# Loads behind the last value stores, one group's first turns ahead of its last scores, and eight row norms beside other units: one edit of a two-layer decoder step

## The chip, the cores and the metric

The kernel runs on one core of one Trainium2 chip. The core has a matrix engine (PE, with its weight loads listed apart as PEld), a vector engine (DVE), a scalar engine (ACT), a general engine (POOL) and a sync engine (SP) that here only issues DMAs. The metric is the time of one execution in device microseconds. The kernel before took 2337.07 us, the median of three runs (2333.03 to 2337.43).

## The reference

One inference step of a two-layer decoder runs over a prompt of 2048 rows and over 8 sequences of 4 new rows with 2048 cached rows each. Model width is 1024. Cut to what the change touches:

```python
# layer 0: HGRN2 heads (a) beside forgetting attention (b), one input and one output projection
proj = rmsnorm(x, norm_even) @ w_in
qa, fa, ia, ga, qb, kb, vb, gb, fb = split(proj)
c = cumsum(log_sigmoid(fb + b_fox))
logits = q @ k.T * scale + c[t] - c[s]          # 4 heads, 128 wide, causal over 2048 rows
o_b = softmax(logits) @ v * silu(gb)            # the new rows attend to paged k, v in the same way
x = x + concat([o_a, o_b]) @ w_out

# layer 1: gated linear attention, 4 heads
h = rmsnorm(x, norm_odd)
q, k, v, g, r = split(h @ w_in_odd)             # here r gives the decay: log_sigmoid(r @ w_gate + b) / 16
o = head_norm(chunked_linear_attention(q, k, v, decay)) * silu(g)
y = rmsnorm(x + o @ w_out_odd, final_norm)
```

The step also returns the keys and values of the prompt and of the new rows, and the final states.

## The kernel before

Products of full precision are made of three half-precision ones: each operand is split in a high and a low half, and `mm3` (lines 603 to 607) issues high by high, high by low and low by high. So a line of PE work shows three lines L605, L606 and L607. Splitting an operand takes one ACT instruction for the high half and one DVE instruction for the low half. The prompt is worked through in two halves of 1024 rows.

The program is written as Python generators. `mux(a, ta, b, tb)` draws from two of them in turn, so that each has used the same part of its planned time `ta` or `tb`; `drain` runs one to its end. A scheduler then sets the order of the instructions on each engine from a simulated timeline. `tc.issue_after(i)` gives it a bound: what is issued inside stands behind instruction `i`. On the chip each engine works its own list in that order, SP too: a DMA issue that waits holds up all later ones.

Three places are touched.

*End of layer 0's input projections.* The last unit computes the values of heads 2 and 3 for the second half. For each pair of row tiles (named by half, head pair and tile: 112 is the pair of tiles 2 and 3) `ev` in `mk_bkv` writes a float tile `Bv`, split halves `Bvs` (ACT line 1048, DVE line 1049), stores `Bvs` to `vd` from SP (line 1063) and `Bv` to the output from POOL (line 1066). Both tiles come from a pool of four buffers, so that the last pair, 116, takes the buffers of 112 and can be written when the stores of 112 have landed.

*Prompt attention, `fox_prompt` (lines 1341 to 1473).* Its 16 groups are 4 heads by 4 stretches of 512 query rows. `loads(h, G)` brings q, k (a transposing DMA), a bias strip, v and a gate strip (names such as `q2_02`: head 0, stretch 2). `scores` makes, for each of four blocks `b` of 128 rows, the products `s` (PE), adds the bias and takes the maximum `mx` (DVE line 1391), the exponentials (ACT line 1399) and the scaling (POOL line 1407). `values` transposes the scores in turns (PE line 1427), splits each turn into `th` (ACT line 1434) and `tl` (DVE line 1435) and multiplies by v into `fo`; it keeps two turns ahead. While group j is scored, the values of group j-1 are drawn, a quarter of them behind each block. The loads of group j+1 are asked for behind block 0 of group j. The last group has no group behind it: its values come by themselves, in two column halves. The decode attention, which reads pages of the cache (`pgcache_fox_k`, transposed by PE line 1546), runs beside the prompt's.

*Layer 1, `phase_odd`.* Units 0 to 7 are layer 0's output projection, and units 8, 9 and 10 are Cv0, Cqk0 and Cg0: head 0's projections for v (with the 16 columns of r), q and k, and gate, over the first half. `three(0, 11)` then runs the recurrences of heads 0 to 2, each beside three later units. Layer 1's rows must be normed before they are projected. `prep(hf)` does this for the 8 row tiles of a half by `norm_store` (lines 521 to 563): load `x1r` from `x1d` (SP line 540), squares `nsq` (ACT line 546), a reciprocal root `rsr` (DVE and POOL), the gain (POOL line 548), the high half (ACT line 553), the low half (DVE line 554), and a store to `xs` (SP line 555). For the second half the `x1r` tiles have two buffers (`yr`), and the loads are bound to stand behind `last_turn`, the last of the transposing DMAs by which `norm_fetch` brings the first half's normed rows from `xs` to `act` (SP line 574). The projection Cv0 writes one row tile at a time to three PSUM buffers; each is free when ACT (line 1884, `vC`) and DVE (`rh`, `rt`) have read it. The end of this part reads:

```python
            self.norm_fetch(act, 0, dense(7, 8))
            fetched(11)
            drain(dense(8, 11))
            drain(mux(prep(1), 10000.0, three(0, 11), 240000.0))
```

Of the kernel before, what the change touches and what calls it, by code (L numbers as in the profile page):

```python
# [111 lines left out]
def drain(g):  # L112
    for _ in g:
        pass
# [11 lines left out]
class Kern:  # L126
# [788 lines left out]
    def even_half(self, hf, act, wpool, wp, pps, npool, S):  # L915
# [104 lines left out]
        def mk_bkv(hp, which):  # L1020
            wide = which == "v" and hp == 0
            width = 260 if wide else 256

            def run(W):
                cs = slice(hp * 256, hp * 256 + 256)
                held = []
                if hf == 0:
                    self.fox_scale(which, hp)

                def ev(ps, g, cnt, m):  # L1030
                    c = sc(f"B{which}{hp}")[:m, 2:3]
                    if wide:
                        tt = hf * 8 + g if m == P else NPG
                        nc.vector.scalar_tensor_tensor(self.lf[:m, tt], ps[:, 0, 256:260], c, self.bfox[:m], ALU.mult,
                                                       ALU.add)
                    if g % 2 == 0:
                        held[:] = [wp.tile([P, 2, 256], F32, tag="c2", name=f"B{which}{hf}{hp}{g}")]
                        if m == P:
                            held.append(wp.tile([P, 512], F32, tag="c2", name=f"B{which}s{hf}{hp}{g}").bitcast(
                                F16).rearrange("p (g h x d) -> p g h x d", g=2, h=2, x=2))  # L1040
                    t = held[0]
                    nc.vector.tensor_scalar(t[:m, g % 2 : g % 2 + cnt], ps[:, :, :256], c, None, ALU.mult)
                    if m == P:
                        u = held[1]
                        for j in range(cnt):
                            src = ps[:, j, :256].rearrange("p (h d) -> p h d", h=2)
                            hi, lo = (u[:, g % 2 + j, :, x] for x in range(2))
                            nc.scalar.activation(hi, src, AF.Copy, scale=self.cu[which, hp])
                            nc.vector.scalar_tensor_tensor(lo, src, self.cu[which, hp], hi, ALU.mult, ALU.subtract)  # L1049
                    if m < P:  # L1050
                        dst = o[f"fox_{which}_s"][0].rearrange("b t h d -> (b t) (h d)")[:, cs]
                        nc.sync.dma_start(dst, t[:m, 0])
                        if which == "v":
                            nc.sync.dma_start(self.vs[:, cs], t[:m, 0])
                    elif (g + cnt) % 2 == 0:
                        if which == "v":
                            x = (hf * 4 + g // 2) * 2 + hp
                            nc.vector.tensor_reduce(self.vmax[:, x : x + 1], t, mybir.AxisListType.XY, ALU.max,
                                                    apply_absolute_value=True)
                        g0 = g // 2 * 2  # L1060
                        pg = hf * 8 + g0
                        dst = {"k": self.kd, "v": self.vd}[which][hf][g0 * P : (g0 + 2) * P, 2 * hp : 2 * hp + 2]
                        nc.sync.dma_start(dst.rearrange("(g s) h x d -> s g (h x d)", s=P),
                                          u.rearrange("p g h x d -> p g (h x d)"))
                        dst = o[f"fox_{which}_p"][0, 0, pg : pg + 2].rearrange("g s h d -> s g (h d)")[:, :, cs]
                        (nc.gpsimd if (hf, hp, which) == (1, 1, "v") else nc.sync).dma_start(dst, t)
                    if which == "k" and m < P:
                        pk = pps.tile([P, 2, 256], F32, tag="gr", name=f"BkT{hf}{hp}{g}")
                        for j in range(2):
                            nc.tensor.transpose(pk[:, j, :m], t[:m, 0, j * P : (j + 1) * P], self.ident[:m, :m])  # L1070
                        ks = wp.tile([P, 2, 256], F32, tag="c2", name=f"BkS{hf}{hp}{g}")
                        nc.scalar.activation(ks[:, :, :m], pk[:, :, :m], AF.Copy, scale=self.fsc["k", hp][0])
                        nc.sync.dma_start(self.ks[2 * hp : 2 * hp + 2].rearrange("h p t -> p h t"), ks[:, :, :m])

                yield from self.proj_tm(pps, act, W, hf, ev, f"B{which}{hf}{hp}", width)

            cols = [({"k": 2560, "v": 3072}[which] + hp * 256, 256)] + ([(4096, 4)] if wide else [])
            U[f"B{which}{hp}"] = unit(cols, f"B{which}{hp}", run)
# [262 lines left out]
    def fox_prompt(self, fx, pps, caus):  # L1341
# [65 lines left out]
                nc.gpsimd.tensor_scalar(lt[:, :w], lt[:, :w], nm[:, 1:2], 2.0**14, ALU.mult, ALU.mult)  # L1407
            return L

        def values(h, G, rows, po, b1, b2):  # L1410

            ns, per = 4 * G + b2, 4 // (b2 - b1)
            c1, c2 = b1 * P, b2 * P
            alone = self.sample_done

            def turn(j):


                tag = "kt" if alone and j % 2 else "t"
                pt = pps.tile([P, 512], F32, tag=tag, name=f"pt{h}{G}{b1}{j}")  # L1420
                w, parts = 0, []
                for s in range(j * per, min(j * per + per, ns)):
                    b0 = max(b1, s - 4 * G)
                    w = max(w, b0 * P if per == 1 else 0)
                    parts.append((s, w, b0 * P))
                    for b in range(b0, b2):
                        nc.tensor.transpose(pt[:, w : w + P], rows[b][s // 4][0][:, (s % 4) * P : (s % 4 + 1) * P],  # L1427
                                            self.ident)
                        w += P
                th = fx.tile([P, 512], F16, tag="th", name=f"th{h}{G}{b1}{j}")  # L1430
                tl = fx.tile([P, 512], F16, tag="tl", name=f"tl{h}{G}{b1}{j}")
                a = parts[0][1]
                self.turns.append((
                    nc.scalar.activation(th[:, a:w], pt[:, a:w], AF.Copy),  # L1434
                    nc.vector.tensor_tensor(tl[:, a:w], pt[:, a:w], th[:, a:w], ALU.subtract)))  # L1435
                return th, tl, parts

            nj = -(-ns // per)
            ahead = [turn(j) for j in range(min(2, nj))]
            for j in range(nj):  # L1440
                if j + len(ahead) < nj:
                    ahead.append(turn(j + len(ahead)))
                th, tl, parts = ahead.pop(0)
                for s, a, c0 in parts:
                    vv = [x[:, s % 4] for x in V[h, s // 4]]
                    self.last_pe = self.mm3(po[:, c0:c2], vv, [x[:, a : a + c2 - c0] for x in (th, tl)], s == 0,
                                            s == ns - 1)
                yield sum(c2 - c0 for _, _, c0 in parts) * 2.1
            y = fx.tile([P, 512], F32, tag="y", name=f"fy{h}{G}{b1}")
            nc.vector.scalar_tensor_tensor(y[:, c1:c2], po[:, c1:c2], self.v_undo[h // 2], SG[h, G][:, c1:c2], ALU.mult,  # L1450
                                           ALU.mult)
            nc.gpsimd.dma_start(self.yT[0][NH + h][:, G * 512 + c1 : G * 512 + c2], y[:, c1:c2])
# [4 lines left out]
        for j, (h, G) in enumerate(groups):  # L1457
            rows = []
            for b in range(4):
                rows.append((yield from scores(h, G, b)))  # L1460
                if j + 1 < len(groups) and b == 0:
                    loads(*groups[j + 1])
                for _ in range(ns // 4):
                    c = next(pv, None)
                    if c:
                        yield c
            yield from pv
            po = pps.tile([P, 512], F32, tag="o", name=f"fo{h}{G}")
            if j + 1 < len(groups):
                pv, ns = values(h, G, rows, po, 0, 4), 4 * (G + 1)  # L1470

        yield from values(h, G, rows, po, 0, 2)
        yield from values(h, G, rows, po, 2, 4)

    def strips(self, makers, sources):

# [497 lines left out]
    def phase_odd(self):  # L1974
# [4 lines left out]
        with pool("act2", side="right") as ap, pool("w2", side="right") as w0, pool("yr2", side="right") as y0, \  # L1979
# [34 lines left out]
            def dense(a, b):  # L2014
                return self.staged(units, a, b)
# [4 lines left out]
            def three(hf, a):  # L2020
                for h in range(3):
                    yield from recur(hf, h, a + 3 * h)
# [70 lines left out]
            drain(mux(prep(0), 11500.0, dense(4, 7), 63000.0))  # L2093
            self.norm_fetch(act, 0, dense(7, 8))
            fetched(11)
            drain(dense(8, 11))
            drain(mux(prep(1), 10000.0, three(0, 11), 240000.0))
            fetched(23)
            self.norm_fetch(act, 1)
            drain(recur(0, 3, 20))  # L2100
# [95 lines left out]
```

## Time and profile before

| what | value |
|---|---|
| median of three runs | 2337.07 us (2333.03 to 2337.43) |
| the profiled execution | 2338.06 us |
| its span | 2336.2 us (so 1.9 us lie around it) |
| granted PE clock, mean | 0.991 |
| PE busy | 2250.3 us, 96% |
| DVE busy | 1448.0 us, 62% |
| ACT busy | 1076.2 us, 46% |
| POOL busy | 768.7 us, 33% |

Times inside the execution are in microseconds from the start of its span. A row of the timeline gives the start, the duration, the engine, the line of the kernel, the operation, the tile written and the tiles read, and in brackets how long the engine had been idle and what ended that. SPq rows are the issues of DMAs; when a DMA lands is told apart. A row of waits gives the instruction that waited, what it waited for, the total, the number of times and the longest.

### The profile page before, as it was taken

To read this page: it belongs to the slowest core of one execution; us is meant where nothing else is said; L and a number is where in the kernel's file an instruction comes from. 1 tells how busy PE (TensorE), PEld (TensorE's weight loads), DVE (VectorE), ACT (ScalarE), POOL (GpSimd) and SP (SyncE) were. 2 spreads that over 40 slices of the span, in tenths; PEclk is the share of its full clock that TensorE was granted. 3 is DMA by queue.
4 is the path that set the end of the run, shared out by engine and by line. 5 is a ranking of instruction groups with operands and counts; after the bars stand their busy time and mean duration, and the time that the engine had idled before them with its cause. 6 is when DMAs were issued, how large, how long until landed. Compare 5 with 4: busy or idle time off the path is not lost.

```text
span 2336.2 us, 58122 instructions
## 1 busy us (share of the span) xinstructions
PE 2250.3 (96%) x23060; PEld 1604.1 (69%) x23060; DVE 1448.0 (62%) x3313; ACT 1076.2 (46%) x2360; POOL 768.7 (33%) x818
## 2 busy tenths in 40 slices
PE   7999999999999989999999999999899999999998
PEld 5667667864655876665545888777677666666887
DVE  7766577537655748667767445366675655557554
ACT  6434344333333326555656543546545545545343
POOL 2333324112212214223335445144552432322232
PEclk9999999999999999999999999999999999999999
DMA  7232334765441278877882968523233431115554
GB/s 201 66 93 67 94 106 152 182 170 138 147 136 43 89 178 268 247 234 221 271 249 73 341 198 261 141 84 119 75 113 86 126 104 58 46 58 163 167 188 150
DMA packets 375665, 344.87 MB, mean 148 GB/s; under 512 B 107633, under 2 KB 322994, under 8 KB 375394
## 3 DMA queue, kind: packets, MB, share of 16 engines
q1 hardware_dynamic: 373250, 334.54, 47.8%
q0 software_dynamic: 2144, 6.62, 0.8%
q8 instruction: 181, 2.97, 0.5%
q14 instruction: 90, 0.74, 0.1%
HBM read 244.54 MB, written 79.63 MB: 139 GB/s over the span
## 4 chain that ended last, share of the span: by engine, by line
PE 78%; DVE 8%; DMA 4%; ACT 3%; issue 2%; POOL 2%; SPq 2%; POOLq 0%; DVEq 0%; ACTq 0%
PE pt_o L605 4%; PE pt_o L607 4%; PE pt_o L606 4%; PE pkt L1546 2%; PE pt L1427 2%; PE pt_Cv L605 2%; PE pt_Cv L606 2%; PE pt_Cv L607 2%; PE sc L1605 1%; PE pv L1684 1%; PE pf_Ag L607 1%; PE pf_Ag L606 1%; PE pf_Ag L605 1%; PE pf_Bq L607 1%; PE pf_Bq L606 1%
## 5 line engine op out<-in xcount | busy, mean ns | idle before, releaser
L605 PE MATMUL pt_o<-w_o,act 128*128 128x256 f16 x1024 | 279.7, 273 | 2.3 <-ACT sg1C L662 2.3
L607 PE MATMUL pt_o<-w_o,act 128*128 128x256 f16 x1024 | 279.6, 273 | 0.9 <-POOL act L1785 0.9
L606 PE MATMUL pt_o<-w_o,act 128*128 128x256 f16 x1024 | 279.6, 273 | 0.0
L605 PEld LDWEIGHTS <-act 128*128 128x128 f16 x2304 | 226.7, 98 | 37.4 <-issue 4.1
L606 PEld LDWEIGHTS <-act 128*128 128x128 f16 x2304 | 226.8, 98 | 32.9 <-issue 3.6
L607 PEld LDWEIGHTS <-act 128*128 128x128 f16 x2304 | 226.8, 98 | 31.4 <-issue 1.9
L606 PE MATMUL pt_Cv<-w_Cv,act 128*128 128x256 f16 (+1 forms) x512 | 141.3, 276 | 0.0
L605 PE MATMUL pt_Cv<-w_Cv,act 128*128 128x256 f16 (+1 forms) x512 | 141.3, 276 | 0.0
L607 PE MATMUL pt_Cv<-w_Cv,act 128*128 128x256 f16 (+1 forms) x512 | 141.2, 276 | 0.0
L772 POOL TENSOR_TENSOR kA<-kA,fA 128x512 f32<-128x512 f32 (+1 forms) x56 | 77.9, 1392 | 186.2 <-PE gl_A L738 140.2
L772 POOL TENSOR_TENSOR kC<-kC,fC 128x512 f32<-128x512 f32 (+1 forms) x56 | 83.9, 1498 | 153.9 <-PE gl_C L738 107.8
L1407 POOL TENSOR_SCALAR L<-L,nm 128x512 f32<-128x512 f32 (+3 forms) x160 | 99.5, 638 | 104.6 <-DVE nm L1403 44.5
L1399 ACT ACTIVATE L<-L,nm,kc 128x512 f32<-128x512 f32 (+3 forms) x160 | 118.2, 741 | 28.9 <-DVE nm L1397 27.6
L1434 ACT ACTIVATE th<-pt 128x512 f16<-128x512 f32 (+3 forms) x159 | 81.6, 528 | 85.1 <-PE pt L1427 82.0
L1435 DVE TENSOR_TENSOR tl<-pt,th 128x512 f16<-128x512 f32 (+3 forms) x159 | 95.0, 608 | 20.3 <-ACT th L1434 18.3
L1427 PE MATMUL pt<-ident,L 128*128 128x128 f32 x544 | 90.6, 278 | 2.1 <-DVE tl L1435 1.1
L1546 PEld LDWEIGHTS pkt<-ident,pgcache_fox_k 128*128 128x128 f32 x512 | 58.9, 142 | 42.9 <-issue 25.6
L1427 PEld LDWEIGHTS pt<-ident,L 128*128 128x128 f32 x544 | 66.4, 142 | 25.8 <-DVE tl L1435 6.2
L1884 ACT ACTIVATE vC<-pt_Cv,kc 128x512 f32<-128x512 f32 (+1 forms) x40 | 23.9, 598 | 130.4 <-PE pt_Cv L607 130.4
L1546 PE MATMUL pkt<-ident,pgcache_fox_k 128*128 128x128 f32 x512 | 77.6, 279 | 6.1 <-DMA pgcache_fox_k<-in_cache_fox_k 1.8
L1374 POOL TENSOR_TENSOR cm<-cb,caus 128x128 f32<-128x128 f32 x64 | 29.1, 456 | 132.1 <-DVE mx L1391 114.4
L605 PE MATMUL pt_Bk<-w_Bk,act 128*128 128x256 f16 x256 | 70.5, 276 | 2.1 <-DVE Bvs L1049 1.8
(959 smaller groups left out, 6750.7 us busy)
## 6 DMA issues: line engine op xcount, KB each, us to landing
pgcache_fox_k<-in_cache_fox_k SPq DMA_DIRECT2D x128, 256.0 KB, 4.2
pgcache_fox_v<-in_cache_fox_v SPq DMA_DIRECT2D x128, 256.0 KB, 4.0
yr<-yT SPq DMA_DIRECT2D x16, 1024.0 KB, 8.1
x1d<-xo SPq DMA_DIRECT2D x44, 256.0 KB, 3.9
wr_Aqf<-in_w_in_even SPq DMA_DIRECT2D x64, 128.0 KB, 3.2
wr_o<-in_w_out_even SPq DMA_DIRECT2D x32, 256.0 KB, 5.3
xo<-in_x_prompt SPq DMA_DIRECT2D x32, 256.0 KB, 5.3
wr_Cv<-in_w_in_odd SPq DMA_DIRECT2D x32, 256.0 KB, 4.0
```

Of the source, the lines that this page charges most:

```text
L605: nc.tensor.matmul(ps, lh[0], rh[0], start=first, stop=False)
L606: nc.tensor.matmul(ps, lh[0], rh[1], start=False, stop=False)
L607: return nc.tensor.matmul(ps, lh[1], rh[0], start=False, stop=last)
L772: nc.gpsimd.tensor_tensor(kv[:, :, 0], kv[:, :, 0], t1.to_broadcast([P, nb, w]), ALU.mult)
L1374: self.last_cm = nc.gpsimd.tensor_tensor(cm, cb[:, tb * P : (tb + 1) * P], caus, ALU.add)
L1399: self.last_exp = nc.scalar.activation(lt[:, :w], lt[:, :w], AF.Exp, bias=nm[:, 0:1], scale=ib, accum_out=nm[:, 2 + j : 3 + j])
L1407: nc.gpsimd.tensor_scalar(lt[:, :w], lt[:, :w], nm[:, 1:2], 2.0**14, ALU.mult, ALU.mult)
L1427: nc.tensor.transpose(pt[:, w : w + P], rows[b][s // 4][0][:, (s % 4) * P : (s % 4 + 1) * P], self.ident)
L1434: nc.scalar.activation(th[:, a:w], pt[:, a:w], AF.Copy),
L1435: nc.vector.tensor_tensor(tl[:, a:w], pt[:, a:w], th[:, a:w], ALU.subtract)))
L1546: last = nc.tensor.transpose(pk[:, j * P : (j + 1) * P], pgs[j][:, h * P : (h + 1) * P], self.ident)
L1884: r = nc.scalar.activation(v[h][:, g : g + cnt], ps[:, :, :256], AF.Copy, scale=c)
```

## The change

The change has three parts, and the instructions stay the same in kind and number.

1. The last store to `vd` is remembered. Behind block 0 of the second group, the loads of the third are bound behind that store; every later group's loads are bound behind the v load of the group before.
2. In the last group, a third of the previous group's values is drawn behind each of the first three blocks. Then `values` for the first column half is begun, which emits its first two turns (transposes, `th`, `tl`) ahead of the scores of the last block. Its products follow behind them.
3. `prep(1)` runs beside units 8, 9 and 10, and `three(0, 11)` by itself.

```diff
-                        nc.sync.dma_start(dst.rearrange("(g s) h x d -> s g (h x d)", s=P),
-                                          u.rearrange("p g h x d -> p g (h x d)"))
+                        self.last_row = nc.sync.dma_start(dst.rearrange("(g s) h x d -> s g (h x d)", s=P),
+                                                          u.rearrange("p g h x d -> p g (h x d)"))
...
-        def values(h, G, rows, po, b1, b2):
+        def values(h, G, rows, po, b1, b2, prime=False):
...
             ahead = [turn(j) for j in range(min(2, nj))]
+            if prime:
+                yield 1
+            po = po()
...
                 if j + 1 < len(groups) and b == 0:
-                    loads(*groups[j + 1])
-                for _ in range(ns // 4):
+                    with ExitStack() as st:
+                        if j == 1:
+                            st.enter_context(self.tc.issue_after(self.last_row.ins))
+                        elif j > 1:
+                            st.enter_context(self.tc.issue_after(self.last_vload.ins))
+                        loads(*groups[j + 1])
+                end = j + 1 == len(groups)
+                for _ in range(ns // (3 if end else 4)):
                     c = next(pv, None)
                     if c:
                         yield c
+                if end and b == 2:
+                    yield from pv
+                    first = values(h, G, rows, lambda: po, 0, 2, True)
+                    next(first)
...
-        yield from values(h, G, rows, po, 0, 2)
-        yield from values(h, G, rows, po, 2, 4)
+        yield from first
+        yield from values(h, G, rows, lambda: po, 2, 4)
...
-            drain(dense(8, 11))
-            drain(mux(prep(1), 10000.0, three(0, 11), 240000.0))
+            drain(mux(prep(1), 10000.0, dense(8, 11), 66000.0))
+            drain(three(0, 11))
```

What the scheduler makes of it is seen in the engines' lists. The first place is SP at the start of prompt attention. Before, from the gate strip of the second group on:

```order
L1368 DMA fsg01_10949<-sgd_79 128x512
L1360 DMA q2_02_11020<-qd_71 128x2x512
L1362 DMA_TRANSPOSE k2_02_11021<-kd1_73 128x2x512
L1353 DMA cb0_10923<-cbd_80 128x512
L1063 DMA vd1_75<-Bvs112_10764 128x2x512
L1364 DMA v2_02_11022<-vd1_75 128x4x256
L1368 DMA fsg02_11027<-sgd_79 128x512
L1362 DMA_TRANSPOSE k2_03_11271<-kd1_73 128x2x512
L1353 DMA cb0_10923<-cbd_80 128x512
L1364 DMA v2_03_11272<-vd1_75 128x4x256
L1362 DMA_TRANSPOSE k2_10_12127<-kd0_72 128x2x512
L1063 DMA vd1_75<-Bvs114_10823 128x2x512
```

And after, from the same row:

```order
L1368 DMA fsg01_10949<-sgd_79 128x512
L1063 DMA vd1_75<-Bvs112_10764 128x2x512
L1063 DMA vd1_75<-Bvs114_10823 128x2x512
L1541 DMA qs_11132<-qs_76 128x4x32
L1541 DMA kn_11133<-ks_77 128x4x32
L1541 DMA sgs_11134<-sgd_79 128x4x32
L1542 DMA vn_11135<-vs_78 32x512
L1063 DMA vd1_75<-Bvs116_10882 128x2x512
L1360 DMA q2_02_11020<-qd_71 128x2x512
L1362 DMA_TRANSPOSE k2_02_11021<-kd1_73 128x2x512
```

The stores of pairs 112 and 114 have moved ahead of the third group's loads, and the store of 116 too, which stood behind the first pages of the cache.

The second place is ACT at the last scores of prompt attention; 315 is head 3's last block, 3300 and 3301 are the first two turns of the last group. Before:

```order
L1399 ACTIVATE L3152_18851,nm315_18860<-L3152_18851,nm315_18860,kc_67 128x512
L1399 ACTIVATE L3153_18857,nm315_18860<-L3153_18857,nm315_18860,kc_67 128x512
L1434 ACTIVATE th3300_18896<-pt3300_18891 128x512
L1434 ACTIVATE th3301_18905<-pt3301_18900 128x512
```

After:

```order
L1399 ACTIVATE L3152_18887,nm315_18896<-L3152_18887,nm315_18896,kc_67 128x512
L1434 ACTIVATE th3300_18855<-pt3300_18850 128x512
L1434 ACTIVATE th3301_18864<-pt3301_18859 128x512
L1399 ACTIVATE L3153_18893,nm315_18896<-L3153_18893,nm315_18896,kc_67 128x512
```

The two turns have moved ahead of one exponential. PE's list is nearly as it was there.

The third place is SP behind the first half's transposes and ACT in Cv0. On SP, before:

```order
L574 DMA_TRANSPOSE act_18820<-xs_84 128x16x128 x7
L334 DMA wr_Cqk01_21743<-in_w_in_odd 128x2x128 x8
L540 DMA x1r10_22103<-x1d_83 128x1024
L540 DMA x1r1128_22573<-x1d_83 128x1024
L334 DMA wr_Cg01_21941<-in_w_in_odd 128x2x256 x4
```

And after:

```order
L574 DMA_TRANSPOSE act_18820<-xs_84 128x16x128 x7
L540 DMA x1r10_21386<-x1d_83 128x1024
L540 DMA x1r1128_21498<-x1d_83 128x1024
L334 DMA wr_Cqk01_21781<-in_w_in_odd 128x2x128 x8
L555 DMA xs_84<-x1r10_21386 128x2048
L334 DMA wr_Cg01_22031<-in_w_in_odd 128x2x256 x3
L540 DMA x1r1256_21579<-x1d_83 128x1024
```

The first two loads of the second half's rows stand right behind the transposes, and the third behind the store of the first row tile. On ACT, Cv0's first evacuations before:

```order
L1884 ACTIVATE vC00_21386<-pt_Cv000_21389,kc_67 128x256
L1884 ACTIVATE vC00_21386<-pt_Cv001_21420,kc_67 128x256
L1884 ACTIVATE vC00_21386<-pt_Cv002_21451,kc_67 128x256
```

After, where the line is 1897:

```order
L1897 ACTIVATE vC00_21388<-pt_Cv000_21391,kc_67 128x256
L546 ACTIVATE nsq0_21500,nss0_21501<-x1r10_21386 128x1024
L1897 ACTIVATE vC00_21388<-pt_Cv001_21422,kc_67 128x256
L546 ACTIVATE nsq128_21581,nss128_21582<-x1r1128_21498 128x1024
L1897 ACTIVATE vC00_21388<-pt_Cv002_21453,kc_67 128x256
```

The squares of the first two row tiles of the second half have come between the evacuations of Cv0's tiles 0, 1 and 2. The later six stand between later evacuations of units 8 to 10.

More of the change, by code (lines that the diff above doesn't have):

```diff
@@ L1469, in fox_prompt @@
             if j + 1 < len(groups):
-                pv, ns = values(h, G, rows, po, 0, 4), 4 * (G + 1)
-        yield from values(h, G, rows, po, 0, 2)
-        yield from values(h, G, rows, po, 2, 4)
+                pv, ns = values(h, G, rows, lambda po=po: po, 0, 4), 4 * (G + 1)
+        yield from first
+        yield from values(h, G, rows, lambda: po, 2, 4)
     def strips(self, makers, sources):
```

## The prediction

> **What bounds the kernel now.** I read the page first, then the waits of PE, then the windows around the three places of the change, and last the timeline of each engine there. The page says that PE carries the kernel:
>
> ```profile
> span 2336.2 us, 58122 instructions
> PE 2250.3 (96%) x23060; PEld 1604.1 (69%) x23060; DVE 1448.0 (62%) x3313; ACT 1076.2 (46%) x2360; POOL 768.7 (33%) x818
> ```
>
> PE is idle for 2336.2 - 2250.3 = 86 us in all. Since no product is taken away, the change can only move that idle time and the stretches in which PE runs at half rate. The waits of PE that the change can reach are these (total, times, longest):
>
> ```profile
> PE s L605 <- DVE mx L1391: 10.0, 8, 8.0
> PE fo L605 <- ACT th L1434: 3.8, 2, 3.0
> PE gl_C L738 <- DVE qC L771: 3.2, 2, 2.7
> ```
>
> The longest, 8.0 us, stands at the start of prompt attention, the second before the last group's products, the third in the stage of the three recurrences. The windows give what each stage has to lose or win (stretch, its length, then busy time of PE, PEld, DVE, ACT and POOL with instruction counts, the granted clock, the DMA share, GB/s):
>
> ```profile
> 855.00:870.00 15.00, 8.12 (x76) 7.14 (x75) 4.38 (x9) 1.51 (x4) 2.88 (x5) 0.87 1.20 261
> 870.00:885.00 15.00, 11.86 (x54) 6.11 (x53) 12.49 (x60) 9.23 (x25) 7.81 (x16) 0.79 1.05 269
> 885.00:900.00 15.00, 14.40 (x93) 9.31 (x94) 12.03 (x38) 8.87 (x20) 8.32 (x21) 0.89 0.93 304
> ...
> 1440.00:1480.00 40.00, 40.00 (x358) 34.86 (x356) 14.45 (x39) 7.97 (x16) 8.72 (x9) 1.00 1.00 235
> ...
> 1540.00:1740.00 200.00, 189.21 (x2361) 142.31 (x2359) 137.54 (x252) 101.64 (x218) 98.35 (x75) 0.99 0.32 102
> ```
>
> In 855 to 900 PE is idle for 45 - 34.38 = 10.6 us and the clock is low; in 1440 to 1480, where Cv0 runs, it has no idle time at all while the DMA engines are full; in 1540 to 1740, where the three recurrences run, it is idle for 10.8 us.
>
> **Part 1, the loads behind the last value stores.** These rows carry the stall:
>
> ```profile
> 862.85 0.27 PE L607 MATMUL s<-k,q 128*128 128x256 f16 x1
> 871.17 0.48 PE L605 MATMUL s<-k,q 128*128 128x384 f16 x1 [8.04 <-DVE mx L1391]
> 873.60 0.63 PE L605 MATMUL s<-k,q 128*128 128x512 f16 x1
> 876.34 0.39 PE L605 MATMUL s<-k,q 128*128 128x512 f16 x1
> 885.42 0.77 PE L1546 MATMUL pkt<-ident,pgcache_fox_k 128*128 128x128 f32 x5 [1.21 <-DMA pgcache_fox_k<-in_cache_fox_k]
> ```
> ```profile
> 868.89 0.47 ACT L1048 ACTIVATE Bvs<-pt_Bv,kc 128x256 f16<-128x256 f32 x1 [9.09 <-DMA vd<-Bvs]
> ```
> ```profile
> 862.74 0.75 DVE L1042 TENSOR_SCALAR Bv<-pt_Bv,kc 128x512 f32<-128x512 f32 x1 [2.43 <-DMA out_fox_v_p<-Bv]
> 870.82 0.28 DVE L1391 CUSTOM_DVE_ANT_0 L<-s,cm 128x128 f32<-128x128 f32 x1
> ```
> ```profile
> 856.07 0.50 SPq L1368 DMA_DIRECT2D fsg<-sgd  x1
> 860.67 0.51 SPq L1063 DMA_DIRECT2D vd<-Bvs  x1
> ...
> 878.31 0.96 SPq L1516 DMA_DIRECT2D pgcache_fox_k<-in_cache_fox_k  x2
> ```
> ```profile
> vd<-Bvs SPq DMA_DIRECT2D x4, 256.0 KB, 6.0
> ```
>
> PE waits for the first maximum on DVE, DVE stands behind the low half of the last value pair, that behind ACT's high half, and ACT waits until 868.89 for the store of pair 112, which frees the buffer. SP issued that store at 860.67, behind q, k and the bias strip of the third group. In the new order it stands right behind the row of 856.07, so it can go at 856.07 + 0.50, about 856.6. With the median landing of 6.0 us it lands at 862.6. But DVE writes the last pair's float tile only from 862.74 on, since its buffer waits for POOL's output store, which is not moved; with its 0.75 us ACT can start at about 863.5, which is 5.4 us earlier. I take 5.3 us off the wait, which leaves 8.04 - 5.3 = 2.7 us. The store of 116 now holds SP until its low half is there: 863.5 and the 1.9 us that lay between ACT's row and DVE's, and some more, about 866. Behind it q2_02, k2_02 and the first four pages are queued. The pages still come earlier than at 878.31, since seven loads of later groups, which stood ahead of them, now stand behind.
>
> The clock counts too. At 873.60 a product of 512 columns takes 0.63 us, at 876.34 the same takes 0.39, so after the stall PE ran at half rate from 871.2 to 876.3: 5.1 us, in which 2.55 us of work were lost. Part 2 shows that a wait of 3 us still costs 3.4 us at half rate, or 1.7 lost, so 0.8 is won. In 885 to 900 the clock is down again (0.89, 1.65 us lost) behind page waits of which the last is 1.21. With pages issued earlier I take a third of these 2.9 us, 0.9. Part 1: -5.3 - 0.8 - 0.9 = -7.0 us. The ends are -10 (all page waits and the second half rate go) and -3 (store 112 lands 2 us late under the full queues, and the page loads wait for k2_02).
>
> **Part 2, the last group's turns.** The rows:
>
> ```profile
> 1268.64 0.27 PE L605 MATMUL fo<-th,v 128*128 128x256 f16 x1 [2.98 <-ACT th L1434]
> 1270.39 0.42 PE L605 MATMUL fo<-th,v 128*128 128x256 f16 x1
> 1272.30 0.27 PE L607 MATMUL fo<-th,v 128*128 128x256 f16 x1
> ```
> ```profile
> 1267.22 0.80 ACT L1399 ACTIVATE L<-L,nm,kc 128x512 f32<-128x512 f32 x1
> 1268.02 1.05 ACT L1434 ACTIVATE th<-pt 128x512 f16<-128x512 f32 x2
> ```
>
> The turns pass one exponential of 0.80 us with its readout, so the products start 0.8 to 0.9 us earlier, and the exponential then ends 1.05 us later; it is wanted only by turns that stand behind these. The half rate behind the wait (0.42 instead of 0.27, until 1272.30) may go with it. I take -0.9; the ends are 0 and -2.5.
>
> [...]
>
> **Part 3, the norms beside Cv0, Cqk0 and Cg0.** The rows:
>
> ```profile
> 1452.00 20.75 SPq L574 DMA_TRANSPOSE act<-xs  x7
> 1472.86 4.11 SPq L334 DMA_DIRECT2D wr_Cqk<-in_w_in_odd  x8
> 1477.06 0.89 SPq L540 DMA_DIRECT2D x1r<-x1d  x2
> ```
> ```profile
> 1472.51 0.47 ACT L1884 ACTIVATE vC<-pt_Cv,kc 128x256 f32<-128x256 f32 x1 [1.46 <-PE pt_Cv L607]
> 1475.40 0.47 ACT L1884 ACTIVATE vC<-pt_Cv,kc 128x256 f32<-128x256 f32 x1 [2.42 <-PE pt_Cv L607]
> ...
> 1511.81 0.54 ACT L662 ACTIVATE sg0C<-pf_C00g,kc 128x352 f32<-128x352 f32 x1
> ```
> ```profile
> L546 ACT ACTIVATE nsq<-x1r x8: 1042/1048/1057, 1530.9 to 1717.6; 128x1024 bf16<-128x1024 f32 x8
> L548 POOL TENSOR_TENSOR x1r<-x1r,grow x8: 2362/2370/2590, 1532.1 to 1718.8; 128x1024 f32<-128x1024 f32 x8
> L553 ACT ACTIVATE x1r<-x1r,rsr_n x8: 1133/1148/1149, 1537.1 to 1723.8; 128x1024 f16<-128x1024 f32 x8
> L554 DVE SCALAR_TENSOR_TENSOR x1r<-x1r,rsr_n x8: 1275/1283/2202, 1538.3 to 1724.9; 128x1024 f16<-128x1024 f32 x8
> DMA to landing us min/median/max: 2.6/3.9/6.6
> ```
> ```profile
> 1632.80 1.38 DVE L554 SCALAR_TENSOR_TENSOR x1r<-x1r,rsr_n 128x1024 f16<-128x1024 f32 x1 [1.63 <-ACT x1r L553]
> ```
> ```profile
> 1636.92 0.69 PE L738 MATMUL gl_C<-qC,kC 128*30 128x16 f32 x62 [2.74 <-DVE qC L771]
> ```
>
> The cost comes first. SP is busy with the transposes until 1452.00 + 20.75 = 1472.75. The load of the first row tile stands behind them, so it goes at 1472.8 and lands 3.9 us later, at 1476.7 (2.6 to 6.6: 1475.4 to 1479.4). ACT's list has the squares of that tile right behind the evacuation of Cv0's tile 0. ACT therefore evacuates nothing from tile 1 on until then, and PE has three PSUM buffers: tiles 1, 2 and 3 fill them. Tile 4 can begin when tile 1 is read: squares 1.05, `vC` 0.47, and 0.7 for the readout and DVE's reading make 1476.7 + 2.2 = 1478.9. Before, tile 4 was evacuated at 1472.51, and a tile takes 1475.40 - 1472.51 = 2.89, so it began at 1469.6. PE stalls for 9.3 us (8.0 to 12.0). Nothing covers it: PE's list has only Cv0's tiles there. A stall of that length cost 2.5 us at half rate in part 1, and I add that.
>
> Then the chain of the later row tiles. With two buffers, a tile's squares, gain, high half, low half, store and the next load take 1.05 + 2.37 + 1.15 + 1.28 + 3.9 + 3.9 = 13.7 us at the least, and each pair of the eight tiles goes through that. The fourth pair is there at 1476.7 + 3 x 13.7 = 1517.8. Its squares stand ahead of Cg0's first evacuation, which was at 1511.81 and will be about 11.8 later, 1523.6. At the median landings there are 5.8 us in hand, at 6.6 us each the pair comes at 1476.7 + 3 x 19.1 = 1534, 10.4 too late. I take 2 us, with 0 and 10.4 as ends.
>
> The gain is in the recurrences. The 2.74 us wait for qC ends when DVE has done two low halves, for which it waited itself (the second is the row of 1632.80); it goes, and with it a half rate of about 3.3 us, 1.6 lost. Of the other 10.8 - 2.74 = 8.1 us most wait for the recurrence's own work; I take 0.7. The ends are 4.3 and the whole, 10.8 + 1.6 = 12.4. Part 3: 9.3 + 2.5 + 2 - 5.0 = +8.8 us.
>
> **Sum.** -7.0 - 0.9 + 8.8 = +0.9 us. Against the profiled execution, 2338.06 (span 2336.2), that makes 2339.0. The median of the runs, 2337.07, lies 1.0 below that execution, so I forecast 2338.0 us. What a measurement of this kernel can tell from no change is about 0.2%, or 4.7 us, and the forecast lies inside.
>
> **Rivals.** *The recurrences win all their idle time.* The norms take 8 x (1.05 + 1.15) us of ACT and 8 x 2.37 of POOL out of that stage, and POOL and DVE are what it waits for. Against it: the other waits there name tiles of the recurrence. Part 3 would be 9.3 + 2.5 - 12.4 = -0.6, the sum -8.5, and the time 2328.6.
>
> *The row tiles' chain holds ACT and PE again and again.* For it speaks that the DMA engines are full in 1440 to 1480 and that `yr` has only two buffers; against it that PE has three PSUM buffers to run ahead in and that the DMA share falls later. It decides from the point where a store and a load together take more than 7.8 + 1.9 us, the 5.8 in hand spread over three rounds. With landings of 6.6 us part 3 is 12.0 + 2.5 + 10.4 - 5.0 = 19.9, the sum +12.0, and the time 2349: slower.
>
> *Attention gains nothing.* SP stands at the store of 116 until about 866, so the third group's k, a transpose, and the pages come when PE is already at them, and the stall moves behind the first scores. For it: the DMA engines are full in 855 to 885 (1.20, 1.05). Against: the seven DMAs that have moved from ahead of the first pages to behind them. Part 1 would be 0, the sum +7.9, and the time 2345.
>
> **How the numbers follow.** The middle case has 0.42: its terms of both signs rest on rows, and their ends lie within about 5 us. The recurrences' full gain has 0.22. The chain has 0.26, since its price hangs on landings under a full queue; attention without gain has 0.10. So faster has 0.22, within 0.2% 0.42, slower 0.36. The middle case alone reaches from 2332 to 2343. The range goes to the rivals' times, 2328 to 2350.
>
> **What would show it.** Part 1 is right if PE's wait for the first maximum is 2 to 4 us and ACT's wait for `vd` is gone. Part 2 shows as a wait for `th` near 2 us. Part 3's cost shows as a PE wait of 8 to 12 us between Cv0's tiles 3 and 4, that ends with ACT's `vC` behind `nsq`, at a clock of 0.5 afterwards. Its gain shows as the missing wait for qC. It would be wrong if the first row tile landed before the transposes end, if the wait at Cv0 came back in Cqk0 and Cg0, or if the recurrences' other waits went as well.

## The result, and the profile after

The changed kernel took 2353.48 us (median of seven runs, 2350.03 to 2364.83); the kernel before took 2334.54 us in seven runs beside it (2330.44 to 2343.57). The ratio is 1.0082, with a 95% interval of 1.0065 to 1.0100: slower by about 19 us, where 2338.0 us with a range of 2328 to 2350 had been forecast. Since then the kernel before has been measured more often; its median was 2331.8 to 2336.1 us in those comparisons, and each ratio below is taken against its runs in the same comparison.

The profiled execution of the changed kernel has a span of 2353.6 us. The waits of PE (total, times, longest):

```profile
PE prT L1912 <- DVE rT L1913: 13.5, 2, 13.3
...
PE zC L1937 <- ACT kC L1956: 5.2, 1, 5.2
PE s L605 <- DVE mx L1391: 5.0, 9, 2.7
...
PE fo L605 <- ACT th L1434: 3.0, 2, 2.2
PE psf L1609 <- ACT lfTs L1608: 2.4, 2, 2.0
```

The wait for the first maximum fell from 8.0 to 2.7 us and the wait for `th` from 3.0 to 2.2. Two new ones stand at the top: 13.3 us in Cv0 and 5.2 us in Cqk0. A third, for `lfTs` in attention, grew from 0.6 to 2.0 us. The 2.7 us wait for qC in the recurrences is gone. The windows (columns as before) show where the time is:

```profile
855.00:870.00 15.00, 11.93 (x94) 8.90 (x92) 8.33 (x31) 4.36 (x11) 4.78 (x11) 0.96 0.88 246
870.00:885.00 15.00, 13.15 (x75) 7.69 (x74) 13.08 (x51) 9.53 (x24) 7.44 (x14) 0.93 1.03 298
...
1440.00:1480.00 40.00, 28.53 (x254) 24.53 (x252) 8.90 (x17) 3.35 (x6) 6.75 (x8) 0.91 1.04 242
1480.00:1500.00 20.00, 17.94 (x143) 13.30 (x144) 14.30 (x31) 11.09 (x21) 9.42 (x7) 0.84 0.48 152
1500.00:1540.00 40.00, 34.68 (x230) 21.57 (x229) 18.38 (x29) 29.91 (x49) 20.35 (x13) 0.91 0.42 140
```

PE is busy for longer in the two windows at the start of attention, 25.1 us against 20.0. In 1440 to 1480, where PE had been busy throughout, 11.5 us are idle, and the clock is 0.91, 0.84 and 0.91 in the three windows from 1440 to 1540.

To see how much each stage gave or took, I compared the starts of the same products in the two traces. The numbers are the median of after less before, in us:

| place | after less before |
|---|---|
| ahead of attention | +0.8 |
| 880 to 890, behind the first scores | -6.2 |
| 895 to 920 | -3.7 |
| 960 to 1130 | -1.9 |
| ahead of the last group's products | -0.8 |
| behind them | -1.7 |
| Cv0, before its wait | -1.2 |
| Cv0, behind it | +14.7 |
| behind Cqk0 | +22.8 |
| end of the three recurrences | +17.2 |
| end | +17.4 |

So the loss is part 3: 24.0 us in units 8 to 10, of which 5.6 come back in the recurrences. Parts 1 and 2 leave 2.0 us of gain against this one trace of before.

The rows of part 3's first wait. ACT and DVE:

```profile
1459.95 0.47 ACT L1897 ACTIVATE vC<-pt_Cv,kc 128x256 f32<-128x256 f32 x1 [19.34 <-PE pt_Cv L607]
1477.73 1.06 ACT L546 ACTIVATE nsq<-x1r 128x1024 bf16<-128x1024 f32 x1 [17.32 <-DMA x1r<-x1d]
...
1478.79 0.45 ACT L1897 ACTIVATE vC<-pt_Cv,kc 128x256 f32<-128x256 f32 x1
```
```profile
1478.91 0.15 DVE L410 TENSOR_SCALAR rst_n<-nss 128x1 f32<-128x1 f32 x1 [17.86 <-ACT nsq L546]
...
1479.54 1.82 DVE L1907 COPY rt<-rh 128x64 f32<-128x64 f32 x1
...
1481.49 0.27 DVE L1913 CAST rT<-prT 80x128 fp32r<-80x128 f32 x1
```
```profile
1481.82 0.44 PE L1912 MATMUL prT<-ident,rt 128*80 128x128 f32 x1 [13.28 <-DVE rT L1913]
```
```profile
1454.43 17.29 SPq L574 DMA_TRANSPOSE act<-xs  x6
1471.81 1.30 SPq L540 DMA_DIRECT2D x1r<-x1d  x2
```

ACT sat 17.3 us for a load that SP could issue only behind the transposes, DVE sat 17.9 us behind ACT's sum, and PE stopped at 1468.55, when tile 3 was done. The last link was a copy of `rT` on DVE, so PE stood at the small transpose for r and not at the PSUM buffer of tile 4. Both hang on the same row of ACT.

The second wait, on ACT:

```profile
1515.39 0.72 ACT L358 ACTIVATE wr_Cv<-wr_Cv,kc 128x512 f32<-128x512 f32 x1 [4.62 <-DMA wr_Cv<-in_w_in_odd]
1518.85 0.72 ACT L358 ACTIVATE wr_Cv<-wr_Cv,kc 128x512 f32<-128x512 f32 x1 [2.73 <-DMA wr_Cv<-in_w_in_odd]
1520.08 1.06 ACT L546 ACTIVATE nsq<-x1r 128x1024 bf16<-128x1024 f32 x1 [0.52 <-DMA x1r<-x1d]
1521.14 0.53 ACT L1956 ACTIVATE kC<-pf_C00k,kc 128x352 f32<-128x352 f32 x1
```

Here the evacuation `kC` stands behind two conversions of weights for a later unit and behind a row tile's squares. ACT sat 4.6 and 2.7 us for the weights and only 0.5 for the row tile. The weights' loads stand on SP among the row tiles' stores and loads, and were issued only just ahead of these waits:

```profile
1508.16 0.34 SPq L555 DMA_DIRECT2D xs<-x1r  x1
1512.43 1.41 SPq L334 DMA_DIRECT2D wr_Cv<-in_w_in_odd  x3
1513.95 0.40 SPq L540 DMA_DIRECT2D x1r<-x1d  x1
1514.39 0.43 SPq L555 DMA_DIRECT2D xs<-x1r  x1
1514.86 0.43 SPq L334 DMA_DIRECT2D wr_Cv<-in_w_in_odd  x1
```
```profile
1506.36 6.04 POOL L360 TENSOR_TENSOR w_Cv<-wr_Cv,w_Cv 128x512 f16<-128x512 f32 x2
```

SP issued the first of these loads when POOL had done the two multiplications that read the weights' buffers. Together they took 6.04 us here, behind a row tile's gain on POOL; in the kernel before the same two took 1.16 and 1.17 us. So this second wait runs from POOL over SP and ACT to PE, and the row tile's own landing is a small part of it.

### The profile page after: what moved, and what is told of

Same layout as the page of the kernel before. It is cut to its first block, busy times and chain, and to the rows that moved or that the text cites. A ratio compares the mean times of both kernels' runs of the same rounds, so it can differ in the third digit from the quotient of the medians.

```text
span 2353.6 us, 58121 instructions
## 1 busy us (share of the span) xinstructions
PE 2257.2 (96%) x23060; PEld 1606.9 (68%) x23060; DVE 1445.8 (61%) x3313; ACT 1075.4 (46%) x2360; POOL 764.0 (32%) x818
## 4 chain that ended last, share of the span: by engine, by line
PE 39%; DVE 4%; DMA 2%; POOL 2%; ACT 2%; issue 1%; SPq 0%; POOLq 0%; DVEq 0%; ACTq 0%
PE pt_o L605 4%; PE pt_o L607 4%; PE pt_o L606 4%; PE pt_Cv L605 2%; PE pt_Cv L606 2%; PE pt_Cv L607 2%; PE o_C L892 1%; PE gl_C L738 1%; PE pt L1427 1%; DMA yr<-yT 1%; DMA x1r<-x1d 1%; PE pv L1697 1%; PE py_C L710 1%; DVE qC L771 0%; DVE scT L753 0%
```

## The experiments

### The parts apart

e1 takes part 3 back:

```diff
-            drain(mux(prep(1), 10000.0, dense(8, 11), 66000.0))
-            drain(three(0, 11))
+            drain(dense(8, 11))
+            drain(mux(prep(1), 10000.0, three(0, 11), 240000.0))
```

> Parts 1 and 2 as in the changed kernel, the second half's norms beside the three recurrences as before. Theory (the whole loss comes from part 3): 2 to 4 us faster than before, since in the trace of the changed kernel PE ran 1.2 to 1.9 us ahead at the end of attention where it had been 0.6 behind at its start; the wait for qC of 2.7 us in the recurrences is back. Rival (the moved loads of attention cost something that the changed trace only hides): slower than before by 3 us or more.

Measured: 2337.86 us against 2335.53, ratio 1.0012 (1.0003 to 1.0022). The theory fell in its sign: the two parts together gain nothing; they cost some 3 us, or little more than nothing. The rival's 3 us lies in the interval's middle. In the profile of e1 PE also waited 1.8 us in Cv0 for the landing of a transposed tile of `act`; whether that is what the runs show is open.

e2 is the kernel before with the two lines of part 3 alone.

> The kernel before with part 3 alone. Theory: 18 to 20 us slower than before, with a PE wait of about 13 us in Cv0 and one of about 5 us in Cqk0. Rival (the parts make each other worse, for instance by the order that the scheduler finds for all of them): under 14 us slower.

Measured: 2354.85 us, ratio 1.0090 (1.0068 to 1.0112), 21 us. Its profile shows the same two waits:

```profile
PE prT L1899 <- DVE rT L1900: 13.4, 2, 12.9
PE s L605 <- DVE mx L1391: 7.6, 8, 5.7
PE zC L1924 <- ACT kC L1943: 5.6, 1, 5.6
```

Part 3 is the whole loss. The middle line is as telling: this kernel has the old order at the start of attention, and its wait there was 5.7 us and not 8.0.

e5 is the kernel before with part 2 alone, e11 with part 1 alone; e5 leaves out the bounds of the loads, e11 the earlier turns.

> The kernel before with part 2 alone (the last group's first turns ahead of its last scores). Theory: the wait for th falls from 3.0 to 2.2 us and the time by about 1 us, which a few runs cannot tell from no change. Rival (the early turns cost more than they bring, and they are what made parts 1 and 2 together 2.8 us slower): 2 to 4 us slower than before.

> The kernel before with part 1 alone. Theory (its wait for the first maximum is 2.7 us in every run against 5.7 to 8.0 with the old order, but the wait for lfTs grows from 0.6 to 2.0 and is followed by half rate): between 3 us below and 3 us above before. Rival (part 1 is worth its 7 us): 5 us or more below.

Measured: e5 2335.93 us, ratio 1.0000 (0.9984 to 1.0016), with a wait for `th` of 2.2 us as in the changed kernel. e11 2333.24 us, ratio 0.9998 (0.9984 to 1.0011). Part 1's rival, 7 us of gain, is out. Part 2 costs nothing that the runs can tell, and its 0.9 us are below that too. Each part alone is level with before, so the 3 us of e1 are not explained by either.

### What the start of attention is worth

e7 is the kernel before, profiled again.

> The kernel before, for a second profile of it. Theory (the 8.0 us wait for the first maximum in the first profile was a long one, since the landing of a store under full DMA queues differs from run to run; with the same order on SP the kernel with part 3 alone showed 5.65): a wait of 5 to 8 us, not the same to 0.1 us as the first. Rival (the place of that wait is set by the order and comes out the same each time): 8.0 us within 0.2.

The waits for the first maximum, of the kernel before again, of e5 (old order there too) and of e11 (new order):

```profile
PE s L605 <- DVE mx L1391: 8.9, 8, 6.9
```
```profile
PE s L605 <- DVE mx L1391: 9.4, 8, 7.5
```
```profile
PE s L605 <- DVE mx L1391: 5.0, 9, 2.7
```

With the old order four profiles show 8.0, 5.7, 7.5 and 6.9 us (mean 7.0); with the new one seven show 2.7: the changed kernel, e1, e3, e4, e8, e9 and e11. From the issue of the store of 112 to ACT's next row took 8.2, 6.5, 7.5 and 7.0 us in the four, so the old wait depends on when a store lands, and the first profile had the longest. In the new wait no DMA is left:

```profile
863.50 0.75 DVE L1042 TENSOR_SCALAR Bv<-pt_Bv,kc 128x512 f32<-128x512 f32 x1 [2.35 <-PE pt_Bv L607]
```

DVE writes the last pair's float tile as soon as PE has made its product, in all seven profiles. The prediction had this row wait for POOL's output store; in the first profile that store came last, but DVE's idle time was 2.43 us and so only 0.08 longer than these 2.35.

The new order pays for it elsewhere. On ACT's list `lfTs2`, a copy that the decode attention's products wait for, now stands behind the four exponentials of the third group's first block; it stood ahead of them. The wait for it is 2.0 us instead of 0.6 in all seven profiles. In the changed kernel the clock was 0.83 from 910 to 920, and a product of 512 columns took 0.63 us instead of 0.38 behind the wait, until 919.5; in the kernel before the clock was 1.00 from 915 to 925. Summed from ahead of attention to 960, against the first trace of before, the kernels with the new order gained 2.3 to 4.3 us (-2.8, -2.7, -4.0, -2.3, -4.2, -4.3 and -2.9), those with the old order 0 (the trace itself), -4.0, +0.4 and -2.1. The means are 3.3 and 1.4 us: part 1 may be worth about 2 us there, which is less than the four old traces differ among themselves, and the runs of e11 say that over the whole kernel it is 0 within some 3 us. Where the rest goes is not settled; the traces differ by 1 to 2 us between 960 and 1320 in both directions.

e6 binds the third group's loads behind the store of 114 alone and binds no later loads; part 2 is in, part 3 is not.

```diff
+                        if g0 == 4:
+                            self.last_row = row
...
-                        elif j > 1:
-                            st.enter_context(self.tc.issue_after(self.last_vload.ins))
```

> Parts 1 and 2 with the norms as before, but the third group's loads are bound behind the store of value pair 114 alone, the later groups' loads are not bound, and ACT's list keeps the two copies lfTs1 and lfTs2 ahead of the exponentials of the third group's first block, as it has them in the kernel before. Theory (with all of part 1, a wait of 2.0 us for lfTs behind four exponentials and the half rate after it take back what the earlier store gives): the first maximum is waited for by 3 to 5 us, the wait for lfTs is 0.6 us, and the time is 0 to 4 us below before. Rival (the start of attention gains nothing from earlier stores, since PE waits for pages and for the clock there): equal to before or 2 to 4 us above.

Measured: 2333.48 us, ratio 0.9988 (0.9977 to 1.0000). The wait for `lfTs` was 0.6 us, and the one for the first maximum 5.4, above what was expected:

```profile
PE s L605 <- DVE mx L1393: 7.7, 9, 5.4
```

In this order ACT still waits for the store of 112 (6.4 us), so the wait hangs on a landing as before: e10 below, with the same start of attention, had 6.1 us. Up to 960 these two traces gained 4.7 and 4.1 us. In the runs e6 has the lowest ratio of the study, 2.8 us below before and at the edge of what they can tell; e10, which adds to it the spread norms, is level with before.

### What holds PE in Cv0

e3 begins the norms beside Cqk0 instead of Cv0:

```diff
-            drain(mux(prep(1), 10000.0, dense(8, 11), 66000.0))
+            drain(dense(8, 9))
+            drain(mux(prep(1), 10000.0, dense(9, 11), 44000.0))
```

> The changed kernel, but the norms begin beside Cqk0 and run beside Cqk0 and Cg0 alone, so that no squares stand between Cv0's evacuations. Theory (the loss is ACT waiting in its list for a row tile's load ahead of an evacuation that PE needs): the 13 us wait is gone, a wait of 0 to 5 us is left behind the later row tiles, whose round trips are now squeezed into two units, and the time is 2 to 8 us below before. Rival (the work of the norms beside dense units is what costs, wherever it begins): still 5 to 15 us slower than before.

Measured: 2342.79 us, ratio 1.0037 (1.0019 to 1.0055). The wait in Cv0 is gone, as the theory had it, but the time is not below before: the rival's range was met. A wait of 8.0 us has come up at the first recurrence, for qC:

```profile
1533.31 1.15 ACT L553 ACTIVATE x1r<-x1r,rsr_n 128x1024 f16<-128x1024 f32 x1 [0.23 <-POOL rsr_n L412]
1536.58 1.06 ACT L546 ACTIVATE nsq<-x1r 128x1024 bf16<-128x1024 f32 x1 [2.13 <-DMA x1r<-x1d]
...
1537.64 1.25 ACT L663 ACTIVATE th_C<-sg1C 128x352 f32<-128x352 f32 x3
```
```profile
1524.10 0.15 DVE L410 TENSOR_SCALAR rst_n<-nss 128x1 f32<-128x1 f32 x1 [3.60 <-ACT nsq L546]
...
1534.66 2.06 DVE L353 SCALAR_TENSOR_TENSOR w_Cg<-wr_Cg,kc,w_Cg 128x512 f16<-128x512 f32 x2
1536.64 1.27 DVE L554 SCALAR_TENSOR_TENSOR x1r<-x1r,rsr_n 128x1024 f16<-128x1024 f32 x1
...
1538.15 2.88 DVE L664 SCALAR_TENSOR_TENSOR sg1C<-th_C,sg1C 128x352 f32<-128x352 f32 x2 [0.17 <-ACT th_C L663]
...
1541.27 1.24 DVE L692 TENSOR_TENSOR qC<-qC,fC 128x1056 f32<-128x1056 f32 x1
```

qC stands on DVE behind the gate's products, these behind ACT's `th_C`, and that behind a row tile's squares that wait for their load. But DVE was idle for only 0.2 us ahead of the gate's products: in PE's 8 us it worked through a split of weights (2.06), a row tile's low half (1.27), the gate's products (2.88) and qC (1.24). It came late to them because it had sat idle before, 3.6 us of it behind a row tile's squares on ACT. So it is in part the same mechanism at another place, and in part the norms' own work, which is what the rival names; how much of each, this run does not show.

e4 lets the first two loads go ahead of the transposes:

```diff
-                if self.last_turn is not None:
+                if self.last_turn is not None and x > 1:
```

> The changed kernel, but the first two row tiles' loads are not bound behind the last transpose; SP has them between the second and the third row tile's transposes instead, some 12 us earlier, and nothing else is changed by hand. Theory (the first stall is the place of these two loads on SP): the wait of 13 us in Cv0 shrinks to under 3 us, the half rate behind it goes, the wait in Cqk0 stays between 0 and 5 us; 2 us faster to 4 us slower than before. Rival (the squares ahead of the evacuations cost by ACT's work or DVE's, not by the load's place): the wait stays over 8 us and the time over 10 us above before.

Measured: 2351.6 us, ratio 1.0063 (1.0042 to 1.0084): 15 us slower, the rival's side. There is no wait of 13 us, but PE waited 3.0, 4.0 and 4.0 us in Cv0, and 1.7 and 0.8 later. With the loads earlier, the scheduler put the squares and the high halves of both tiles ahead of all of Cv0's evacuations:

```profile
1467.12 1.06 ACT L546 ACTIVATE nsq<-x1r 128x1024 bf16<-128x1024 f32 x1 [21.68 <-DMA x1r<-x1d]
...
1471.26 1.15 ACT L553 ACTIVATE x1r<-x1r,rsr_n 128x1024 f16<-128x1024 f32 x1 [1.66 <-POOL rsr_n L412]
1475.07 1.15 ACT L553 ACTIVATE x1r<-x1r,rsr_n 128x1024 f16<-128x1024 f32 x1 [2.66 <-POOL rsr_n L412]
1476.12 1.19 ACT L1897 ACTIVATE vC<-pt_Cv,kc 128x256 f32<-128x256 f32 x3
...
1489.30 1.06 ACT L546 ACTIVATE nsq<-x1r 128x1024 bf16<-128x1024 f32 x1 [8.52 <-DMA x1r<-x1d]
```

So the place of the two loads on SP is not the cause by itself. What holds PE is the order on ACT and DVE: steps of the norms, which wait for DMA and POOL, stand ahead of evacuations that PE waits for. (The first of the three waits ended with DVE's `xo`, an evacuation of layer 0's output projection behind both tiles' reciprocal roots.)

e9 gives Cv0 five PSUM buffers and flips r later:

```diff
-                        if len(waiting) > 1:
+                        if len(waiting) > (4 if hf == 0 else 1):
...
+                banks = ("pj", "o", "pj") if (hf, h) == (0, 0) else ("pj",)
```

> The changed kernel, but Cv0 of the first half has five PSUM buffers instead of three (two of the recurrences' output buffers, free there) and its small transposes prT come three tiles later in PE's list. ACT's list is the same up to tile 6. Theory (PE stops because ACT, held by the row tile's load, gives no PSUM buffer back; the wait is the time that the load is late less what PE can run ahead): PE runs two tiles further, 5.8 us, and the first wait is 6 to 9 us instead of 13.3; the time 3 to 8 us below the changed kernel. Rival (PE is held by the small transposes or by act's own transposes, not by PSUM): a first wait of 12 us or more.

Measured: 2350.48 us, ratio 1.0076 (1.0048 to 1.0104). The first wait was 8.2 us, in the range of the theory: PE ran two tiles further. The time did not follow: its ratio cannot be told from the changed kernel's 1.0082. PE waited again at the end of Cv0, 4.8 us for `rt` of the few rows, with 1.0, 0.5, 0.5 and 1.7 us beside it, since the flips that had been put off and the row tiles' steps stood ahead of them on DVE. All waits of PE from Cv0 to Cg0 add up to 16.8 us against 18.7 in the changed kernel, so running ahead mostly moved them.

e8 multiplies the second half's row tiles by the gain on DVE instead of POOL (in line 548).

> The changed kernel, but the second half's row tiles are multiplied by the gain on DVE instead of POOL. In the changed kernel DVE's small copies rt took 1.8 to 2.3 us instead of 0.2 while POOL multiplied a row tile. Theory (most of the first wait is the load and the order on ACT; this contention is 2 to 4 us of it): copies of 0.2 us, a first wait of 10 to 12 us instead of 13.3, and the time 2 to 8 us below the changed kernel. Rival (POOL's and DVE's contention is the main cost): a first wait under 8 us and a time within 6 us of before.

Measured: 2348.82 us, ratio 1.0050 (1.0033 to 1.0067), which is 7 us less than the changed kernel's ratio gives. The first wait was 9.8 us, with one of 2.0 for `act` ahead of it, and the one in Cqk0 was 1.0. In the two traces units 8 to 10 lose 21.2 us instead of 24.0, so about 3 of the 7 us lie there. POOL's gain is part of the loss, and not the main part.

### A slower draw

e10 is e6 with the norms spread over Cqk0, Cg0 and all three recurrences.

```diff
+            drain(dense(8, 9))
+            def both():
+                yield from dense(9, 11)
+                yield from three(0, 11)
+            drain(mux(prep(1), 10000.0, both(), 284000.0))
```

> The kernel of the store of 114, with the second half's norms spread from Cqk0 over Cg0 and all three recurrences (a step for each tenth of that stretch), so that a third of them leaves the recurrences. Theory (a norm step costs where it stands ahead of what PE needs, and one at a time costs 1 to 3 us): no wait over 3 us in Cqk0 and Cg0, the wait for qC of 2.7 us in the recurrences may go or stay, and the time is within 4 us of the kernel of the store of 114. Rival (any norm step beside dense units stops PE for long): a wait over 5 us in Cqk0 or Cg0 and 5 us or more above before.

Measured: 2334.59 us against 2331.77, ratio 1.0005 (0.9989 to 1.0020). No wait over 0.4 us stands in Cqk0 or Cg0; the wait for qC stayed:

```profile
PE gl_C L738 <- DVE qC L771: 3.2, 2, 2.8
```

Two row tiles' squares fall beside Cqk0 and Cg0 here, and they cost PE nothing that shows; in the changed kernel eight fall into some 70 us from Cv0 on.

## Why the prediction was wrong

**Part 1: the wait right, the gain not there.** The wait left was forecast at 2.7 us and is 2.7. But the term of -7.0 measured 0 (0.9998, interval about 3 us to each side). The failing steps are two. "I take 5.3 us off the wait" took the 8.04 us of one profile for the wait of the kernel; the same order gave 5.7, 6.9 and 7.5 in others. And "I take a third of these 2.9 us" looked for gains in what follows, while the new order of ACT's list, which the prediction did not take up there, brought the wait for `lfTs` of 2.0 us. In the trace the changed kernel stood 7.0 us better right behind the first scores, as much as was forecast; 2.5 of these were lost again by 895 and 1.8 more by 960, the latter behind that wait. The rival that attention gains nothing came true by another mechanism than the one I gave it: PE did not wait for k, and for pages 1.5 us up to 945 against 1.8 before.

**Part 2: right.** 2.1 us were forecast to be left, 2.2 are; the products stood 0.9 us earlier in the trace, which is too little for the runs to show.

**Part 3: the place and mechanism of the first wait and of the gain right, the cost about half.** The cost was put at 9.3 + 2.5 + 2 = 13.8 us and came to 24.0 in the trace; the gain at 5.0, and came to 5.6.
- First wait: 13.3 instead of 9.3. It began where it was forecast. "lands 3.9 us later" was the mis-sized step: the load took 5.9 us, from 1471.81 to 1477.73. I had taken the median of a stage with the DMA engines a third busy (share 0.32) for a place where they are full (1.04). "make 1476.7 + 2.2" was short too: 4.1 us passed from the landing to PE's start, since DVE's copy of `rt` took 1.82 us, and it and the copy of `rT` were in the chain. So the wait did not end with `vC`, as the sign in the prediction had it, but one step later on DVE. The half rate cost what was taken (2.6, the 15.9 us between the table's two rows of Cv0 less the wait's 13.3, against 2.5): Cv0's products took 0.43 us instead of 0.28 until 1486.4.
- The row tiles' chain: "I take 2 us" against 8.1 (a wait of 5.2, the half rate behind it, with a clock of 0.77 from 1515 to 1530, and smaller waits). The round trip was set at 13.7 us, from durations and median landings alone. The squares of each pair's first tile started at 1477.73, 1496.90, 1520.08 and 1536.83: rounds of 19.2, 23.2 and 16.8 us. The wait stood at the third pair, in Cqk0, and not at the fourth, in Cg0. And most of it came for weights that SP issues among the row tiles' transfers and POOL's multiplications hold up, which I had left out. No run moves these loads alone, so their share of the 8.1 us is not shown.
- The gain in the recurrences was right in size and place, and e10 shows the wait for qC coming back with the norms.

**The sum and the range.** The rival in which the chain holds PE came nearest, and its part 3 of 19.9 us is close to the 18.4 of the trace and the 21 of e2. In part that is luck: it set the chain at 10.4 us by slow landings of the row tiles, and what held PE there were mostly the weights. Its time of 2349 was still 4.5 us short, and the range with it, 3.5 us, because it carried parts 1 and 2 at -7.9 us, as the middle case and the first rival did. Only the rival of 0.10 left part 1 out, and it had part 3 at +8.8. A gain from one trace stood in the other cases as if it were certain.

## What to carry to other kernels

On engines that work their list in order, ask of each moved instruction what stands right behind it: a step that waits for a DMA is dear when an evacuation for PE is next (13.3 us here), and here more buffers for PE (16.8 us of waits instead of 18.7) or an earlier load (15 us slower than before instead of 19) mostly moved that wait. When a term is the length of one wait in one trace, and a landing at a DMA share of 1.2 ends it, give it the spread of several executions (5.7 to 8.0 us here), and let the rivals do without it. Take landings from the rows of the same place and the same DMA share, not from a median over a quiet stage (5.9 us at a share of 1.04 here, against a median of 3.9 at 0.32).

## What the hardware showed that was not expected

DVE's copy `rt` of 128x64 elements, which takes 0.20 us, took up to 2.27 us while POOL multiplied a row tile of 128x1024:

```profile
1481.81 2.35 POOL L548 TENSOR_TENSOR x1r<-x1r,grow 128x1024 f32<-128x1024 f32 x1
```
```profile
1481.94 2.27 DVE L1907 COPY rt<-rh 128x64 f32<-128x64 f32 x1
```

The copy began just behind POOL's multiplication and ended with it, at 1484.2. The tile's view, of the changed kernel (min, median, max in ns) and of e8, where DVE does that multiplication:

```profile
L1907 DVE COPY rt<-rh x8: 195/196/2275, 1460.7 to 1498.7; 128x64 f32<-128x64 f32 x8
```
```profile
L1907 DVE COPY rt<-rh x8: 180/194/796, 1459.1 to 1496.5; 128x64 f32<-128x64 f32 x8
```

With the row tiles' gain off POOL the longest was 0.80 us. The two other long copies of the changed kernel, of 1.82 and 1.83 us, also ended within 0.1 us of POOL's multiplication of a row tile. Why a copy takes longer beside it, no run shows.

PE fell to half rate behind a wait of 2.18 us, one product and a second wait of 0.46 us:

```profile
1267.08 0.27 PE L605 MATMUL fo<-th,v 128*128 128x256 f16 x1 [2.18 <-ACT th L1434]
1267.81 0.27 PE L606 MATMUL fo<-tl,v 128*128 128x256 f16 x1 [0.46 <-DVE tl L1435]
...
1268.43 0.42 PE L607 MATMUL fo<-th,v 128*128 128x256 f16 x1
...
1271.54 0.27 PE L605 MATMUL fo<-th,v 128*128 128x256 f16 x1
```

So the earlier turns of part 2 shortened the wait and kept the half rate. From 1268.0 to 1271.5 the products took 0.42 us instead of 0.27 and started 0.21 us apart instead of 0.11, so these 2.2 us of waiting cost an estimated 1.7 us more.
